# Router of a two-block network on one core: tokens split before the norm's root is known, the root applied per expert slot

## The chip, the cores and the metric

One NeuronCore of a Trainium2 chip runs the whole network in one launch. The metric is device time in microseconds (us) of that launch. The engines that matter here are TensorE (PE; its weight loads are PEld), VectorE (DVE), ScalarE (ACT), GpSimd (POOL) and SyncE (SP), whose queue issues the weight transfers.

## The reference, cut to what matters

A first network block (two layers) and a hybrid attention layer run over 256 tokens of width 1024; then comes a mixture of experts with 32 experts of hidden width 512, two per token, and a last norm. Only the way into the experts is touched:

```python
def rms_norm_2(x, g):
    y = x * lax.rsqrt(jnp.mean(x * x, axis=-1, keepdims=True) + RMS_EPS)
    return y * g

x = x + mixed @ w_out
x = x + hier_moe(rms_norm_2(x, g_ffn), ...)

def hier_moe(xt, ...):
    g_logit = xt @ w_group + b_group            # 4 groups: the best one is taken
    e_logit = xt @ w_expert + b_expert          # 8 experts in it: the best two are taken
    ...
    hid = jax.nn.silu(xb @ w1[e]) * (xb @ w3[e])
    out = hid @ w2[e]                           # weighted by the gate, summed per token
```

The norm's factor (the reciprocal root) is one number per token, so it can be applied to the logits and to the products with w1 and w3 in place of the tokens themselves.

## The kernel before

**Stages.** The tokens stand in two halves b = 0, 1 of 128 tokens, one per partition; `h` is the residual. The output projection (`work`, three fp32r matmuls per product, L122 to L124) fills four PSUM banks `accs[b][n]`, n being the half of the 1024 columns. Then, per half of the tokens: `half(b, n)` adds the bank to `h`, squares it (ACT) and multiplies by the norm's gain into `ys[b]` (GpSimd for n = 0, VectorE for n = 1); `scale(b)` makes the reciprocal root `rs[b]`; `turned(b, n)` transposes `ys[b]` and copies it to `yT` (ACT, L1210); `logits(b, n)` multiplies by the router's weights; `choose(b)` picks the two experts in twelve VectorE instructions (L1184 to L1195); `kept(b)` puts `h` back into the PSUM banks; and `place(b)` splits the normed tokens into a high and a low part `xs[0]`, `xs[1]` (tiles `xt`): the high part on ACT (L1237), the low part on GpSimd (L1242). ACT, VectorE and GpSimd run these in the order in which the code calls them (`ordered`). After `choose(1)` come the ranks within each expert (five small matmuls), `rank`, and the experts.

**Experts.** `pairs` goes over 16 pairs of experts, each expert with 64 slots. `where` compares ranks and makes the one-hot `oh` (L1392); `gather` multiplies `xs` by it into `xg` (PE, L1407); `up` multiplies by w1 and w3 (L1420), `silu` and `product` (L1352) give `hid`, `turn` transposes it (L1356), `down` multiplies by w2 (L1438), `collect` adds the result to the tokens (L1445). `slots` transposes the gates (L1426) into `GT` and the slot's gate `gs`. All engines but SP run this in the written order (`in_order`).

**Weights.** Each pair needs six loads of 2048 KB (two of w1, w3, w2 each), all issued by SP in order. They go to eleven slots (names `mw` and `w`); the twelfth load takes the place of the first one, so it waits until the matmuls of `up` with the first tile are done. Load number k+11 in general waits for the last reader of load k.

Of the kernel before, what the change touches and what calls it, by code (L numbers as in the profile page):

```python
# [56 lines left out]
class Net:  # L57
# [1108 lines left out]
    def to_moe(self):  # L1166
# [30 lines left out]
        def go(accs, work):  # L1197
# [20 lines left out]
            def half(b, n):  # L1218
                sl = slice(n * 512, (n + 1) * 512)
                yield v.tensor_add(h[:, b, sl], h[:, b, sl], accs[b][n])  # L1220
                self.square(h[:, b, sl], ss[b], n)
                yield (nc.gpsimd, v)[n].tensor_mul(ys[b][:, sl], h[:, b, sl], self.gp[:, sl])
# [3 lines left out]
            def kept(b):  # L1226
                for n in range(2):
                    nc.tensor.matmul(accs[b][n], self.ident, h[:, b, n * 512:(n + 1) * 512], start=True, stop=False)

            def scale(b):  # L1230
                yield self.rstd_begin(ss[b])
                yield rs.append(self.rstd_end(ss[b]))
# [17 lines left out]
            with self.ordered():  # L1250
                run(half(0, 0))
                run(half(0, 1))
                run(scale(0))
                for n in range(2):
# [91 lines left out]
    def silu(self, h1, hid):  # L1346
# [3 lines left out]
    def product(self, h3, hid):  # L1350
        hv = hid.rearrange("q c p -> q p c")
        self.nc.vector.tensor_mul(hv, hv, h3.rearrange("q (p c) -> q p c", c=4))  # L1352
# [27 lines left out]
    def pairs(self, ps):  # L1380
# [42 lines left out]
        def slots(q, og):  # L1423
# [3 lines left out]
            GT, gs = self.t(self.ex, (T,), FR, "GT", 2), self.small(1, "gs", bufs=2)  # L1427
            v.tensor_scalar(GT, gp, 0.0, None, op0=OP.is_gt)
            v.reduce_sum(gs, gp, axis=AX.X)
            return GT, gs  # L1430
# [16 lines left out]
        before = None  # L1447
        oh, xg = where(ps[0] // 2), A((8, 256), "xg")
        if ps[0] == 0:
            self.gates(A((4, 128), "hT")[:, 0, :64])  # L1450
            self.spill(A((4, 128), "hid")[:, 0, :64].rearrange("p (r e) -> p r e", r=2))
        og = gated(ps[0] // 2, oh)
        for p in ps:
            g, q = divmod(p, 2)
            more = q == 1 and p != ps[-1]
            if more:
                oh = where(g + 1)
            hid, hT = A((4, 128), "hid"), A((4, 128), "hT")
# [35 lines left out]
    def overflowing(self, wt, ps, oh, og, xg, hid, hT):  # L1494
# [5 lines left out]
        rs, gs, i2 = self.small(2), self.small(2), self.small(8, "i2", I32, 1)  # L1500
# [233 lines left out]
```

## Time and profile before

| | us |
|---|---|
| median of 3 runs (1306.73 to 1308.27) | 1306.81 |
| the profiled execution's own time | 1308.52 |
| its span, first to last instruction | 1306.7 |
| busy: PE / DVE / ACT / POOL | 1242.1 / 692.2 / 598.9 / 169.2 |

The 1.8 us between the span and the execution's own time lie outside the program's instructions. PE is counted busy while a matmul waits in its pipeline too, so its share does not say that PE is the limit everywhere. The output projection ends and the router starts at about 836 us of the span; the experts take from about 859 to 1296 us.

### The profile page before, as it was taken

To read this page: it belongs to the slowest core of one execution; us is meant where nothing else is said; L and a number is where in the kernel's file an instruction comes from. 1 tells how busy PE (TensorE), PEld (TensorE's weight loads), DVE (VectorE), ACT (ScalarE), POOL (GpSimd) and SP (SyncE) were. 2 spreads that over 40 slices of the span, in tenths; PEclk is the share of its full clock that TensorE was granted. 3 is DMA by queue.
4 is the path that set the end of the run, shared out by engine and by line. 5 is a ranking of instruction groups with operands and counts; after the bars stand their busy time and mean duration, and the time that the engine had idled before them with its cause. 6 is when DMAs were issued, how large, how long until landed. Compare 5 with 4: busy or idle time off the path is not lost. (4 is left out here: it accounts for less than half of the span.)

```text
span 1306.7 us, 19148 instructions
## 1 busy us (share of the span) xinstructions
PE 1242.1 (95%) x7647; PEld 922.7 (71%) x7647; DVE 692.2 (53%) x1396; ACT 598.9 (46%) x1113; POOL 169.2 (13%) x174
## 2 busy tenths in 40 slices
PE   7899999999999999999989999979999999989896
PEld 6787999997997899998888899734344343433332
DVE  5778977776787887777578645641111111111112
ACT  5667655555776755556445655431111111111103
POOL 4101000003021000001564511310000000000000
PEclk9999999999999999999989999989999999999999
DMA  9544555393452475344523375789999999999995
GB/s 370 220 160 147 199 190 183 107 339 118 161 194 81 149 257 194 130 159 141 210 78 117 130 257 201 288 326 414 427 427 428 427 427 427 428 426 427 427 423 228
DMA packets 93175, 341.05 MB, mean 261 GB/s; under 512 B 6972, under 2 KB 14108, under 8 KB 69788
## 3 DMA queue, kind: packets, MB, share of 16 engines
q1 hardware_dynamic: 91680, 336.87, 65.4%
q10 hardware_dynamic: 1404, 2.93, 0.7%
q8 instruction: 61, 1.00, 0.3%
q14 instruction: 30, 0.25, 0.0%
HBM read 338.75 MB, written 1.05 MB: 260 GB/s over the span
## 5 line engine op out<-in xcount | busy, mean ns | idle before, releaser
L122 PE MATMUL ps<-xt,wh 128*128 128x256 f32 x1072 | 303.0, 283 | 0.0
L124 PE MATMUL ps<-xt,wl 128*128 128x256 f32 x1072 | 300.6, 280 | 0.2 <-DVE wl L117 0.2
L123 PE MATMUL ps<-xt,wh 128*128 128x256 f32 x1072 | 300.2, 280 | 0.0
L117 DVE TENSOR_TENSOR wl<-w,wh 128x1024 fp32r<-128x1024 f32 (+3 forms) x193 | 228.0, 1187 | 96.3 <-ACT wh L116 95.0
L116 ACT ACTIVATE wh<-w 128x1024 fp32r<-128x1024 f32 (+2 forms) x196 | 197.2, 1014 | 164.9 <-PE ps L123 130.8
L122 PEld LDWEIGHTS ps<-xt,wh 128*128 128x128 f32 x1072 | 202.0, 188 | 4.0 <-issue 1.4
L123 PEld LDWEIGHTS ps<-xt,wh 128*128 128x128 f32 x1072 | 202.1, 189 | 1.9
L124 PEld LDWEIGHTS ps<-xt,wl 128*128 128x128 f32 x1072 | 201.9, 188 | 1.1 <-DVE wl L117 0.6
L1420 PE MATMUL ps<-mw,xg 128*64 128x512 f32 x592 | 132.3, 597 | 5.3 <-DMA mw<-in_w_dram 5.3
L1352 DVE TENSOR_TENSOR hid<-hid,ps 128x512 f32<-128x512 f32 x16 | 17.1, 1068 | 217.0 <-PE ps L1420 198.7
L1420 PEld LDWEIGHTS ps<-mw,xg 128*64 128x64 f32 x592 | 42.4, 138 | 91.0 <-issue 80.7
L1440 DVE SCALAR_TENSOR_TENSOR ys<-ps,gs,ys 128x512 fp32r<-128x512 f32 x32 | 24.0, 751 | 152.7 <-ACT ys L1439 152.7
L1420 PE MATMUL ps<-w,xg 128*64 128x512 f32 x432 | 96.3, 594 | 6.5 <-DMA w<-in_w_dram 6.5
L226 POOL TENSOR_TENSOR nu<-h,gain 128x512 f32<-128x512 f32 x18 | 25.7, 1450 | 428.6 <-DVE h L298 367.4
L1420 PEld LDWEIGHTS ps<-w,xg 128*64 128x64 f32 x432 | 30.7, 137 | 69.6 <-issue 58.5
L1439 ACT ACTIVATE ys<-ps,gs 128x512 fp32r<-128x512 f32 x32 | 22.0, 687 | 106.4 <-PE ps L1438 106.4
L124 PE MATMUL ps<-dh,hT 128*128 128x512 f32 x176 | 69.4, 394 | 0.0
L122 PE MATMUL ps<-dh,hT 128*128 128x512 f32 x176 | 69.3, 396 | 0.0
L123 PE MATMUL ps<-dl,hT 128*128 128x512 f32 x176 | 68.7, 391 | 0.0
L1357 ACT ACTIVATE hT<-ps 128x512 f32<-128x512 f32 x16 | 9.6, 598 | 126.2 <-PE ps L1356 126.1
L116 ACT ACTIVATE dh<-w 128x1024 fp32r<-128x1024 f32 x44 | 46.1, 1056 | 45.7 <-PE ps L124 44.0
L117 DVE TENSOR_TENSOR dl<-w,dh 128x1024 fp32r<-128x1024 f32 x44 | 53.8, 1223 | 22.4 <-ACT dh L116 22.4
(413 smaller groups left out, 2195.9 us busy)
## 6 DMA issues: line engine op xcount, KB each, us to landing
mw<-in_w_dram SPq DMA_DIRECT2D x49, 2048.0 KB, 28.8
w<-in_w_dram SPq DMA_DIRECT2D x41, 2048.0 KB, 27.2
w<-in_ffn_w_up_dram SPq DMA_DIRECT2D x20, 2048.0 KB, 7.9
w<-in_w_in_dram SPq DMA_DIRECT2D x11, 2048.0 KB, 7.4
w<-in_ffn_w_down_dram SPq DMA_DIRECT2D x10, 2048.0 KB, 7.7
w<-in_diff_w_qkv_dram SPq DMA_DIRECT2D x6, 2048.0 KB, 8.1
mw<-in_w_dram SPq DMA_DIRECT2D x6, 1024.0 KB, 18.3
w<-in_mla_w_o_dram SPq DMA_DIRECT2D x2, 2048.0 KB, 16.6
```

Source lines behind the costliest of these rows:

```text
L116: self.nc.scalar.activation(v(hi), raw, AF.Copy)
L117: (eng or self.nc.vector).tensor_sub(v(lo), raw, v(hi).bitcast(FT))
L122: mm(out, a[0], b[0], start=start, stop=False)
L123: mm(out, a[0], b[1], start=False, stop=False)
L124: mm(out, a[1], b[0], start=False, stop=stop)
L226: x = eng[n].tensor_mul(w[n], self.h[:, b, sl], self.gp[:, sl])
L1352: self.nc.vector.tensor_mul(hv, hv, h3.rearrange("q (p c) -> q p c", c=4))
L1357: self.nc.scalar.activation(hT.rearrange("p c s -> p (c s)"), pt, AF.Copy)
L1420: mm(p[64 * z:64 * z + 64], xg[:, k, c0:c0 + 64], wt[k // 4][:, o:o + 512], start=k == 0, stop=k == 7)
L1439: nc.scalar.activation(ys[0][n], p, AF.Copy, scale=gs)
L1440: v.scalar_tensor_tensor(ys[1][n], p, gs, ys[0][n].bitcast(FT), op0=OP.mult, op1=OP.subtract)
```

## The change

The tokens are split without the root: `high` and `low` take `ys` (residual times gain) by halves of the columns, before the root is known, so `place` with its four long instructions goes away; `low` stands on VectorE for three of the four halves and on GpSimd for (0, 1). Only the router's logits get the root (in `choose`, as before). `choose(0)` now stands ahead of `half(1, 1)` on VectorE instead of behind and within it. The root is kept in `self.rstd`; `row_scales` spreads it over all partitions once (two small matmuls, tile `rb`), `row_scale` sums it per slot (VectorE, one instruction per pair), and `silu` and `product` multiply by it. `slots` is called one pair ahead, and for the first pair between the w1 and the w3 products.

```diff
-            def place(b):
-                yk = ys[b].rearrange("q (p k) -> q k p", k=8)
-                hi, lo = self.xs[0][:, b], self.xs[1][:, b]
-                nc.scalar.activation(hi, yk, AF.Copy, scale=rs[b])
-                if b:
-                    nc.scalar.activation(ys[b], ys[b], AF.Copy, scale=rs[b])
-                else:
-                    nc.gpsimd.tensor_scalar(ys[b], ys[b], rs[b], None, op0=OP.mult)
-                nc.gpsimd.tensor_sub(lo, yk, hi.bitcast(FT))
+            def part(b, n):
+                yk = ys[b][:, n * 512:(n + 1) * 512].rearrange("q (p k) -> q k p", k=8)
+                return [yk] + [x[:, b, :, 64 * n:64 * n + 64] for x in self.xs]
+
+            def high(b, n):
+                yk, hi, _ = part(b, n)
+                nc.scalar.activation(hi, yk, AF.Copy)
+
+            def low(b, n, eng):
+                yk, hi, lo = part(b, n)
+                eng.tensor_sub(lo, yk, hi.bitcast(FT))
...
-                run(half(0, 0))
-                run(half(0, 1))
-                run(scale(0))
-                for n in range(2):
-                    turned(0, n)
-                run(half(1, 0))
-                place(0)
+                half(0, 0)
+                half(0, 1)
+                high(0, 0)
+                turned(0, 0)
+                turned(0, 1)
+                half(1, 0)
+                low(0, 0, v)
+                scale(0)
+                high(0, 1)
                 work(1, (1,), (5,))
                 for n in range(2):
                     logits(0, n)
+                scaled(0)
+                run(choose(0, lp, rs[0]))
+                low(0, 1, nc.gpsimd)
                 turned(1, 0)
-                work(1, (1,), (6,))
+                high(1, 0)
+                work(1, (1,))
                 logits(1, 0)
-                work(1, (1,))
-                c0 = choose(0, lp, rs[0])
-                run(half(1, 1))
-                for _ in range(5):
-                    next(c0)
-                run(scale(1), c0)
-                kept(0)
+                kept(0, 0)
+                half(1, 1)
+                scale(1)
+                low(1, 0, v)
                 turned(1, 1)
+                scaled(1)
+                high(1, 1)
                 logits(1, 1)
-                kept(1)
-                place(1)
+                kept(0, 1)
+                for n in range(2):
+                    kept(1, n)
                 run(choose(1, lp, rs[1]))
+                low(1, 1, v)
...
+                self.rstd = self.small(2, "rstd", bufs=1)
+                for b in range(2):
+                    v.tensor_copy(self.rstd[:, b:b + 1], rs[b])
...
-        self.nc.scalar.activation(hv, h1.rearrange("q (p c) -> q p c", c=4), AF.Silu)
+        self.nc.scalar.activation(hv, h1.rearrange("q (p c) -> q p c", c=4), AF.Silu, scale=r)
...
-        self.nc.vector.tensor_mul(hv, hv, h3.rearrange("q (p c) -> q p c", c=4))
+        self.nc.vector.scalar_tensor_tensor(hv, h3.rearrange("q (p c) -> q p c", c=4), r, hv, op0=OP.mult, op1=OP.mult)
+
+    def row_scale(self, gT, r):
+        j = self.t(self.ex, (T,), BF, "rj", 1)
+        self.nc.vector.scalar_tensor_tensor(j, gT, 0.0, self.rb, op0=OP.is_gt, op1=OP.mult, accum_out=r)
+        return r
+
+    def row_scales(self, dg):
+        p = self.ps()[:, :T]
+        for b in range(2):
+            self.nc.vector.tensor_scalar(dg[:, b], self.ident, self.rstd[:, b:b + 1], None, op0=OP.mult)
+        self.nc.gpsimd.memset(dg[:, 2], 1.0)
+        for b in range(2):
+            self.nc.tensor.matmul(p[:, b * 128:(b + 1) * 128], dg[:, 2], dg[:, b], start=True, stop=True)
+        self.rb = self.t(self.ex, (T,), FT, "rb", 1)
+        self.nc.scalar.activation(self.rb, p, AF.Copy)
...
+            h1 = up(q, xg, oh if p == ps[0] else None)
+            if p == 0:
+                self.row_scales(dg)
+                self.spill(A((4, 128), "hT")[:, 0, :64].rearrange("p (r e) -> p r e", r=2))
+            if now is None:
+                now = slots(q, og)
+            GT, gs, r = now
...
+            if p != ps[-1]:
+                now = slots(1 - q, og)
             wt = self.weights()
```

Below is VectorE's queue around `half(1, 1)`, the add and the gain of the last quarter (L1220 and L1222, bank `ps_9334`, tile `y_1672`). First as it stood before:

```order
L1220 TENSOR_TENSOR h_88<-h_88,ps_9334 128x512
L1222 TENSOR_TENSOR y_1672_9311<-h_88,gain_6955 128x512
L1184 SCALAR_TENSOR_TENSOR lg_83<-ps_9425,sm_9429,br_8616 128x36
L1185 TENSOR_REDUCE gm_9321<-lg_83 128x1
L1186 SCALAR_TENSOR_TENSOR sm_9323<-lg_83,gm_9321,sm_9313 128x4
L1187 TENSOR_REDUCE sm_9318<-sm_9323 128x1
L1188 TENSOR_SCALAR sm_9324<-sm_9323,sm_9318 128x4
L161 TENSOR_SCALAR sm_9430<-sm_9430 128x1
```

The same place in the changed kernel, from the end of `choose(0)` on:

```order
L1194 TENSOR_SCALAR one_9316<-consts_92,sm_9326 128x32 x2
L1195 TENSOR_TENSOR asg_9315<-one_9316 128x32
L1220 TENSOR_TENSOR h_88<-h_88,ps_9334 128x512
L1222 TENSOR_TENSOR y_1672_9311<-h_88,gain_6955 128x512
L161 TENSOR_SCALAR sm_9430<-sm_9430 128x1
L165 TENSOR_SCALAR sm_9430<-sm_9430 128x1
L1246 TENSOR_TENSOR xt_1711_9428<-y_1672_9311,xt_1710_9427 128x8x64
L172 RECIPROCAL sm_9430<-sm_9430 128x1
L173 SCALAR_TENSOR_TENSOR sm_9430<-sm_9430 128x1
L174 SCALAR_TENSOR_TENSOR sm_9430<-sm_9430 128x1
L1184 SCALAR_TENSOR_TENSOR lg_83<-ps_9425,sm_9430,br_8616 128x36
```

The first token half's choice moved from behind the last quarter's add to ahead of it; `low(1, 0)` (L1246) is new between the two steps of the root.

The end of VectorE's router work, before; L1282 makes `rank`, L1392 the one-hot `oh`:

```order
L1194 TENSOR_SCALAR one_9316<-consts_92,sm_9326 128x32 x2
L1195 TENSOR_TENSOR asg_9315<-one_9316 128x32
L1282 SCALAR_TENSOR_TENSOR rank_81<-ps_9426,asg_9315 128x64
L1392 TENSOR_TENSOR oh_9615<-rank_81,consts_92 128x256 x2
L1293 TENSOR_TENSOR sm_9620<-lg_83,gm_9321 128x8
```

And in the changed kernel, where the rank is on L1293 and the one-hot on L1421:

```order
L1194 TENSOR_SCALAR one_9316<-consts_92,sm_9326 128x32 x2
L1195 TENSOR_TENSOR asg_9315<-one_9316 128x32
L1246 TENSOR_TENSOR xt_1711_9428<-y_1672_9311,xt_1710_9427 128x8x64
L1293 SCALAR_TENSOR_TENSOR rank_81<-ps_9426,asg_9315 128x64
L1299 COPY rstd_9587<-sm_9429 128x1
L1299 COPY rstd_9587<-sm_9430 128x1
L1421 TENSOR_TENSOR oh_9620<-rank_81,consts_92 128x256 x2
```

`low(1, 1)` and two copies of the root came in between the choice and the one-hot.

TensorE's queue in the first pair of experts, before, from the second half of the w1 product to the first w2 product:

```order
L1420 MATMUL ps_9658<-mw_8608,xg_9618 64x512 x8
L1420 MATMUL ps_9720<-w_9716,xg_9618 64x512 x8
L1420 MATMUL ps_9720<-w_9718,xg_9618 64x512 x8
L1426 MATMUL ps_9738<-consts_92,og_9653 128x128 x2
L1356 MATMUL ps_9745<-consts_92,hid_9656 128x128 x4
L1438 MATMUL ps_9755<-w_9751,hT_9657 64x512 x4
```

And in the changed kernel (L1449 is the `up` matmul, L1455 the gates' transpose, L1385 that of `hid`, L1468 the `down` matmul):

```order
L1449 MATMUL ps_9646<-mw_8608,xg_9623 64x512 x8
L1379 MATMUL ps_9703<-hid_9642 128x128 x2
L1455 MATMUL ps_9727<-consts_92,og_9643 128x128 x2
L1449 MATMUL ps_9744<-w_9740,xg_9623 64x512 x8
L1449 MATMUL ps_9744<-w_9742,xg_9623 64x512 x8
L1385 MATMUL ps_9762<-consts_92,hid_9737 128x128 x4
L1455 MATMUL ps_9768<-consts_92,og_9643 128x128 x2
L1468 MATMUL ps_9782<-w_9778,hT_9738 64x512 x4
```

Two matmuls of the root (L1379) are new ahead of the w3 product, the gates' transposes moved there from behind it, and those of the next pair came in ahead of `down`.

## Rows read from the trace of the kernel before

**Rows 1.** Windows: a stretch of the expert stage, with the view's columns.

```profile
core 0: us, PE busy (x) PEld busy (x) DVE busy (x) ACT busy (x) POOL busy (x), PEclk, DMA share, GB/s
1200.00:1250.00 50.00, 44.58 (x219) 18.23 (x220) 5.50 (x9) 7.83 (x11) 3.31 (x4) 1.00 1.01 427
```

**Rows 2.** Windows of 2 us around the start of the experts, same columns.

```profile
854.00:856.00 2.00, 0.00 (x0) 0.00 (x0) 1.93 (x5) 1.82 (x2) 1.38 (x1) 0.53 1.03 438
...
862.00:864.00 2.00, 2.00 (x8) 0.92 (x8) 1.76 (x10) 0.60 (x1) 0.88 (x2) 0.50 0.00 0
864.00:866.00 2.00, 2.00 (x10) 0.56 (x8) 0.06 (x1) 0.00 (x0) 0.00 (x0) 0.91 0.00 0
...
888.00:890.00 2.00, 2.00 (x14) 0.59 (x10) 0.00 (x0) 0.65 (x1) 0.00 (x0) 1.00 0.89 320
```

**Rows 3.** Timeline of SP's queue: start, us from first to last issue, loads.

```profile
846.92 20.61 SPq L1339 DMA_DIRECT2D mw<-in_w_dram  x2
...
876.28 11.71 SPq L1337 DMA_DIRECT2D w<-in_w_dram  x3
```

**Rows 4.** Chain that ended last, in order of time: start, us, what.

```profile
1121.53 32.80 DMA w<-in_w_dram
...
1286.93 0.22 PE ps L1426 x2
```

**Rows 5.** Timeline, all engines, from the last quarter's add to the experts.

```profile
845.44 0.69 DVE L1220 TENSOR_TENSOR h<-h,ps 128x512 f32<-128x512 f32 x1 [5.08 <-PE ps L124]
846.17 0.69 DVE L1222 TENSOR_TENSOR y<-h,gain 128x512 f32<-128x512 f32 x1
846.51 3.05 POOL L1242 TENSOR_TENSOR xt<-y,xt 128x1024 fp32r<-128x1024 f32 x1
847.25 2.33 DVE L1186 SCALAR_TENSOR_TENSOR sm<-lg,gm,sm 128x4 f32<-128x4 f32 x1
850.39 0.58 ACT L1210 ACTIVATE yT<-ps 128x512 f32<-128x512 f32 x1
851.02 1.08 PE L1214 MATMUL ps<-wr,yT 128*128 128x36 f32 x8 [1.67 <-ACT yT L1210]
852.28 0.25 DVE L1184 SCALAR_TENSOR_TENSOR lg<-ps,sm,br 128x36 f32<-128x36 f32 x1
852.76 0.22 DVE L1186 SCALAR_TENSOR_TENSOR sm<-lg,gm,sm 128x4 f32<-128x4 f32 x1
854.44 3.06 DVE L1194 TENSOR_SCALAR one<-consts,sm 128x32 bf16<-128x32 f32 x2
854.62 2.84 POOL L1242 TENSOR_TENSOR xt<-y,xt 128x1024 fp32r<-128x1024 f32 x1 [5.05 <-ACT y L1239]
857.53 0.17 DVE L1195 TENSOR_TENSOR asg<-one 128x32 bf16<-128x32 bf16 x1
858.36 0.76 DVE L1392 TENSOR_TENSOR oh<-rank,consts 128x256 fp32r<-128x256 f32 x2
858.93 3.75 PE L1407 MATMUL ps<-oh,xt 128*128 128x256 f32 x16 [0.93 <-DVE oh L1392]
862.62 4.50 PE L1420 MATMUL ps<-mw,xg 128*64 128x512 f32 x16
```

**Rows 6.** Timeline of the same kernel, PE and ACT, just ahead of that.

```profile
840.63 1.87 PE L1214 MATMUL ps<-wr,yT 128*128 128x36 f32 x16
...
841.29 2.19 ACT L1237 ACTIVATE xt<-y,sm 128x1024 fp32r<-128x1024 f32 x1
...
844.93 0.48 PE L124 MATMUL ps<-wh,mix 128*128 128x512 f32 x1
```

**Rows 7.** Groups of instructions by line and form: busy us, mean ns.

```profile
L1352 DVE TENSOR_TENSOR hid<-hid,ps 128x512 f32<-128x512 f32 x16 | 17.1, 1068 | 217.0 <-PE ps L1420 198.7 <-issue 18.2
L1242 POOL TENSOR_TENSOR xt<-y,xt 128x1024 fp32r<-128x1024 f32 x2 | 5.9, 2946 | 5.1 <-ACT y L1239 5.1
```

**Rows 8.** Timeline of PE in the first pair, the gates' transposes.

```profile
879.60 0.44 PE L1426 MATMUL ps<-consts,og 128*128 128x128 f32 x2
```

More of the change, by code (lines that the diff above doesn't have):

```diff
@@ L1219, in half, with kept, scaled, run @@
                 sl = slice(n * 512, (n + 1) * 512)
-                yield v.tensor_add(h[:, b, sl], h[:, b, sl], accs[b][n])
+                v.tensor_add(h[:, b, sl], h[:, b, sl], accs[b][n])
                 self.square(h[:, b, sl], ss[b], n)
-                yield (nc.gpsimd, v)[n].tensor_mul(ys[b][:, sl], h[:, b, sl], self.gp[:, sl])
+                (nc.gpsimd, v)[n].tensor_mul(ys[b][:, sl], h[:, b, sl], self.gp[:, sl])
             self.accs = accs
-            def kept(b):
-                for n in range(2):
-                    nc.tensor.matmul(accs[b][n], self.ident, h[:, b, n * 512:(n + 1) * 512], start=True, stop=False)
+            def kept(b, n):
+                nc.tensor.matmul(accs[b][n], self.ident, h[:, b, n * 512:(n + 1) * 512], start=True, stop=False)
             def scale(b):
-                yield self.rstd_begin(ss[b])
-                yield rs.append(self.rstd_end(ss[b]))
-            def place(b):
-                yk = ys[b].rearrange("q (p k) -> q k p", k=8)
-                hi, lo = self.xs[0][:, b], self.xs[1][:, b]
-                nc.scalar.activation(hi, yk, AF.Copy, scale=rs[b])
-                if b:
-                    nc.scalar.activation(ys[b], ys[b], AF.Copy, scale=rs[b])
-                else:
-                    nc.gpsimd.tensor_scalar(ys[b], ys[b], rs[b], None, op0=OP.mult)
-                nc.gpsimd.tensor_sub(lo, yk, hi.bitcast(FT))
-            def run(*gs):
-                for _ in itertools.zip_longest(*gs):
+                self.rstd_begin(ss[b])
+                self.root(ss[b])
+            def scaled(b):
+                rs.append(self.rstd_end(ss[b], True))
+            def part(b, n):
[7 more added lines that the diff above has]
+                eng.tensor_sub(lo, yk, hi.bitcast(FT))
+            def run(g):
+                for _ in g:
                     pass
@@ L1344, in wslot, with silu, product @@
         return t
-    def silu(self, h1, hid):
+    def silu(self, h1, hid, r):
         hv = hid.rearrange("q c p -> q p c")
-        self.nc.scalar.activation(hv, h1.rearrange("q (p c) -> q p c", c=4), AF.Silu)
-    def product(self, h3, hid):
+        self.nc.scalar.activation(hv, h1.rearrange("q (p c) -> q p c", c=4), AF.Silu, scale=r)
+    def product(self, h3, hid, r):
         hv = hid.rearrange("q c p -> q p c")
-        self.nc.vector.tensor_mul(hv, hv, h3.rearrange("q (p c) -> q p c", c=4))
+        self.nc.vector.scalar_tensor_tensor(hv, h3.rearrange("q (p c) -> q p c", c=4), r, hv, op0=OP.mult, op1=OP.mult)
[12 more added lines that the diff above has]
+        self.nc.scalar.activation(self.rb, p, AF.Copy)
     def turn(self, hid, hT, pt):
@@ L1426, in slots @@
                 nc.tensor.transpose(gp[:, b * 128:(b + 1) * 128], og[:, b, 2 * q:2 * q + 2].rearrange("p e s -> p (e s)"), self.ident)
-            GT, gs = self.t(self.ex, (T,), FR, "GT", 2), self.small(1, "gs", bufs=2)
+            GT, gs, r = self.t(self.ex, (T,), FR, "GT", 2), self.small(1, "gs", bufs=2), self.small(1, "rg", bufs=2)
+            self.row_scale(gp, r)
             v.tensor_scalar(GT, gp, 0.0, None, op0=OP.is_gt)
             v.reduce_sum(gs, gp, axis=AX.X)
-            return GT, gs
+            return GT, gs, r
         def down(hT, wt, n, gs, last):
@@ L1445, in collect @@
                     mm(accs[b][n], GT[:, b * 128:(b + 1) * 128], ys[x][n], start=False, stop=last and x == 1)
-        before = None
+        before, now = None, None
         oh, xg = where(ps[0] // 2), A((8, 256), "xg")
@@ L1450, in pairs @@
             self.gates(A((4, 128), "hT")[:, 0, :64])
-            self.spill(A((4, 128), "hid")[:, 0, :64].rearrange("p (r e) -> p r e", r=2))
+            dg = A((4, 128), "hid")
         og = gated(ps[0] // 2, oh)
@@ L1457, in pairs @@
                 oh = where(g + 1)
+                og = gated(g + 1, oh)
+            h1 = up(q, xg, oh if p == ps[0] else None)
[5 more added lines that the diff above has]
+            GT, gs, r = now
             hid, hT = A((4, 128), "hid"), A((4, 128), "hT")
-            h1 = up(q, xg, oh if p == ps[0] else None)
-            self.silu(h1, hid)
+            self.silu(h1, hid, r)
             h3 = up(q, xg, None)
-            self.product(h3, hid)
+            self.product(h3, hid, r)
             if before:
@@ L1499, in overflowing @@
         tmp, t2 = hT[:, 0, :32], [self.small(8) for _ in range(2)]
-        rs, gs, i2 = self.small(2), self.small(2), self.small(8, "i2", I32, 1)
+        rs, gs, i2, r = self.small(2), self.small(2), self.small(8, "i2", I32, 1), self.small(1)
         e = nc.sync.value_load(ei[0:1, 0:1], min_val=0, max_val=31)
@@ L1528, in overflowing @@
                 mm(ps[z], xg[:, k], wt[z][:, k * 512:(k + 1) * 512], start=k == 0, stop=k == 7)
-        self.silu(ps[0], hid)
-        self.product(ps[1], hid)
+        self.silu(ps[0], hid, r)
+        self.product(ps[1], hid, r)
         self.turn(hid, hT, ps[3])
```

5 lines of the change are left out of this document (1 added, 4 removed).

## Prediction

> **What bounds the kernel now.** I read the windows of the last third first. While the experts run, the DMA share is 1.01 and 427 GB/s arrive [rows 1]: the weights' transfers are the limit, and TensorE, busy 44.58 of 50 us there, waits for them in the end. The chain of waits says how far ahead the loads are: one issued at 1121.53 landed 32.80 us later, where a load of 2048 KB takes 4.9 us at 427 GB/s, so several stood in line and a late release of one slot cost nothing [rows 4]. From such a point on the end is fixed by bytes over rate. What can move it is a hole in the transfers before the line has formed.
>
> Windows of 2 us find it: nothing moves from 862 to 866 us [rows 2]. SP's queue says why. It issued the eleventh load at 846.92 and the twelfth 20.61 - 0.37 us later (the last issue itself takes 0.37), at 867.16 [rows 3]. The twelfth takes the place of the first, which TensorE reads in its first w1 product from 862.62 for 4.50 us [rows 5]. So **whatever brings the first gather and that product forward by x us brings all later loads, and the end, forward by x**, as long as the eleven loads are not themselves late: they end at about 862, some 5 us ahead of the release.
>
> The timeline gives the path there [rows 5]. The last quarter's add on VectorE starts at 845.44, once the output projection's last matmul (844.93 + 0.48) is done [rows 6]; the gather starts at 858.93, 13.49 us later. Two VectorE steps stick out: L1186, 0.22 us at 852.76, took 2.33 at 847.25, and the pair L1194 took 3.06. Both end with an L1242 of GpSimd, 846.51 + 3.05 and 854.62 + 2.84. The first of them also held back the root on ACT, and behind it the copy L1210: y of the quarter was done at 846.86 and its copy began only at 850.39.
>
> **The change, part by part.** All times count from T, the start of the last quarter's add, which is 845.44 before.
>
> *Where T goes.* `choose(0)` now stands ahead of that add, so T is its end. The logits of the first half are done at 840.63 + 1.87 = 842.5 [rows 6]. L1184 and L1185 follow (0.25 and about as much), so L1186 is due at about 843.1. `low(0, 1)` on GpSimd becomes ready at the same time: ACT was free for L1237 at 841.29 and now does there the root (0.3, an estimate from the one-column steps of these rows) and `high(0, 1)`, half of 2.19; the other `high` ahead of it mostly fills idle time: about 843.0. GpSimd then runs half of L1242's 2946 ns [rows 7], 1.5 us, to 844.5. I expect VectorE to be held again for that time. What is left of `choose(0)` behind L1186 is, in `choose(1)` of before, 854.44 - 852.98 = 1.46 up to L1194, 0.4 for its pair unheld (two such as L1186) and 0.17, so 2.05 us [rows 5]. T is about 846.6, **1.15 us later** than before. Bounds: 846.0 if L1186 gets in first, 847.6 under the second rival.
>
> *From T to the gather.* y of the quarter is done at T + 1.42 as before (846.17 + 0.69 - 845.44). The root no longer waits behind L1186, so the four transposes (0.22 each [rows 8], so 0.9) and the copy (0.58) give T + 2.9, the logits (1.08) T + 4.0. `low(1, 0)` on VectorE lies beside this: no row shows a VectorE subtraction with this stride; its bounds are 0.69 (plain 512 columns, L1222) and 1.07 (L1352, 512 columns with a stride) [rows 5, 7]. I take 1.07, since both are strided; the root is then done at T + 3.7, still ahead of the logits, so it costs nothing. `choose(1)` unheld takes 852.98 - 852.28 = 0.70 and 2.05, so T + 6.8; GpSimd has nothing to do there. New on the path: `low(1, 1)`, 1.07 (bounds as above), and two copies of one column (0.17 each, as L1195, the shortest row). The ranks' matmuls hide behind `low(1, 1)`. With the rank (0.25) that is T + 8.5 for the one-hot, and the gather starts 858.93 - 858.36 = 0.57 after it: **T + 9.1 in place of T + 13.49, 4.4 us shorter**. With T the gather starts at about 855.7, 3.2 us earlier. The gather and the first product are not changed, so the release of the first slot moves by the same 3.2.
>
> *The clock.* TensorE idles from the last logits (851.02 + 1.08) to 858.93 but for five small matmuls; the granted clock is 0.53 in 854 to 856 and still 0.50 in 862 to 864, then 0.91 [rows 2], so it fell to the lower level (1.2 GHz) in the gap and came back about 5.4 us after the gather began. The gap is now 5.1 us (T + 4.0 to T + 9.1), shorter, so I expect it to fall again, with a slow stretch of work that is 0 to 1 us shorter, worth half of it: 0.4 with some rounding up.
>
> *Given back in the first pair.* Between the w1 and the w3 products TensorE now also does the two root matmuls and two gate transposes. The transposes are 0.44 [rows 8]; the matmuls of the same size 0.25 to 0.6, I take 0.4. The transposes that follow `turn` lie beside ACT's copy of `hid`. So `down` ends 0.8 us later relative to the gather. That counts: the third load of the group at 876.28 was issued at its end, 887.6 [rows 3], it waits for the first slot that `down` frees, and DMA already sags there, to 320 GB/s in 888 to 890 [rows 2]. The line has not formed yet. **0.8 us lost.** The loads in front have 3 us of cover or more, since the DMA is behind them.
>
> *Nothing elsewhere.* In later pairs VectorE does one more instruction of 256 columns and a three-operand product; it is busy for 5.50 of 50 us in the expert stage [rows 1], and SP has loads in line [rows 4]. If that cover were gone each pair would cost up to about 0.5 us. At the end of the last pair the gates' transposes are gone from between the w3 product and `turn`: 0.22 gained [rows 4].
>
> *Sum.* 4.4 - 1.15 + 0.4 - 0.8 + 0.2 = 3.05, so 3.0 us less. The profiled execution took 1308.52 (span 1306.7), 1.7 over the median of 1306.81; both should move alike: 1305.5 for such an execution, **1303.8 as the median**.
>
> **The rivals.**
> (1) *The clock stays up or returns early.* For it: the gap is 1.7 us shorter. Against: a gap of 5.1 us is still long. The first gathers (3.75 us at half clock) and the start of the product (4.50) would save up to 2.4 us in all [rows 5], 2.0 beyond my 0.4: 1301.8.
> (2) *VectorE and GpSimd meet once more.* The new subtractions read two SBUF tiles, and `low(0, 0)` is due just as GpSimd starts the gain of (1, 0). If GpSimd is first, the subtraction, the root behind it and `choose(0)` slip by about 0.9; if the subtractions cost more than 1.07, some tenths more. Gain 1.6 to 2.1: 1305.0. The Trainium skill, page "SBUF — State Buffer", section "Who interferes with whom", says that a VectorE instruction with two SBUF inputs and a GpSimd instruction that reads SBUF exclude each other, the first to start holding for its whole length. By that rule the change brings one meeting of this kind back into `choose(0)` and a second into `low(0, 0)`; the trace agrees as far as L1186 shows it, 2.33 us for 0.22. Without the rule, with GpSimd free for VectorE, T would be near 845.3 and the gain about 4.
> (3) *No change.* The w3 product waits for the new root work (VectorE's scaling of the identity, GpSimd's fill), some 3 us in place of 0.8. Against it: both are due some 10 us before the w1 product ends. 1306.8.
> (4) *Slower.* `low(0, 1)` on GpSimd takes far longer in its new three-level form than half of L1242, and holds VectorE and with it T. My sum is used up when it takes 4.5 us, and the kernel is slower by 0.2% from 7.1 on; at 8 us it would be 1310.3. L1242 with the same stride speaks against it.
>
> **How the numbers follow.** About 0.2%, 2.6 us, is what a measurement of this kernel can tell from no change. Forecast 45% (its own range 1302.9 to 1304.9; some two thirds of it are over 2.6 us of gain), rival 1 18%, rival 2 22%, rival 3 8%, rival 4 7%. Faster is 0.30 from the forecast, 0.18 from rival 1 and 0.04 from the better end of rival 2: 0.52. Same is the rest of the forecast and of rival 2 and rival 3: 0.41. Slower is rival 4, 0.07. The range of 8 in 10 runs from 1301.6 (the clock and plain-price subtractions) to 1306.3 (most of rival 2 and a part of rival 3).
>
> **What would show it.** In the profile after: the first gather at about 855.7 and the twelfth issue at about 863.7; no VectorE step of the router over 1.1 us behind T; one of `choose(0)` held until GpSimd's `low(0, 1)` ends; T near 846.6; a low clock until about 5 us after the gather begins; the w3 product 0.8 us behind the w1 product; DMA at 427 GB/s from about 890 to the end. I am wrong if the gather comes forward and the twelfth issue does not, or if both do and holes open in DMA after 890.

## The result, and the profile after

The changed kernel takes 1315.13 us (median of 4 runs, 1313.84 to 1316.02) and the kernel before 1306.77 (4 runs, 1306.08 to 1308.27): a ratio of 1.0065, 95% interval 1.0053 to 1.0078. It is slower by 0.65%, outside the range of the forecast. The profiled execution shown here took 1313.84 (span 1312.1). It is the fastest of its four, and that of the kernel before, 1308.52, is slower than all four of its kernel, so the two traces differ by 5.3 us where the medians differ by 8.4.

The timeline of the changed kernel around the router answers to [rows 5]. L1246 is `low`, L1186 the step of four columns, L1436 the gather, L1449 the product:

```profile
840.84 0.69 DVE L1220 TENSOR_TENSOR h<-h,ps 128x512 f32<-128x512 f32 x1 [0.82 <-PE ps L124]
...
847.52 1.63 POOL L1246 TENSOR_TENSOR xt<-y,xt 128x512 fp32r<-128x512 f32 x1 [0.58 <-ACT xt L1242]
848.11 1.07 DVE L1186 SCALAR_TENSOR_TENSOR sm<-lg,gm,sm 128x4 f32<-128x4 f32 x1
...
851.14 0.68 DVE L1220 TENSOR_TENSOR h<-h,ps 128x512 f32<-128x512 f32 x1
...
855.61 0.22 DVE L1186 SCALAR_TENSOR_TENSOR sm<-lg,gm,sm 128x4 f32<-128x4 f32 x1
...
857.79 1.06 DVE L1246 TENSOR_TENSOR xt<-y,xt 128x512 fp32r<-128x512 f32 x1
...
859.59 3.75 PE L1436 MATMUL ps<-oh,xt 128*128 128x256 f32 x16 [1.43 <-DVE oh L1421]
863.27 4.11 PE L1449 MATMUL ps<-mw,xg 128*64 128x512 f32 x16
```

From T, the start of the last quarter's add (851.14), to the gather it is 8.45 us, where 13.49 were before and 9.1 forecast. So the router did what it should. Yet the gather starts at 859.59, later than before. The first line says why: the router's first add stands at 840.84. Before, the same row was:

```profile
836.01 0.69 DVE L1220 TENSOR_TENSOR h<-h,ps 128x512 f32<-128x512 f32 x1 [0.83 <-PE ps L124]
```

So 4.83 us were lost ahead of the router, in code that the diff does not touch. SP's queue in the changed kernel (start, us from first to last issue, loads; answers to [rows 3]):

```profile
852.61 15.19 SPq L1353 DMA_DIRECT2D mw<-in_w_dram  x2
...
877.56 11.78 SPq L1351 DMA_DIRECT2D w<-in_w_dram  x3
...
1307.06 2.06 SPq L1609 DMA_DIRECT2D out_dram<-mw  x4
```

The twelfth load went out at 852.61 + 15.19 - 0.37 = 867.43, and the output's first store at 1307.06. Before, that store stood at

```profile
1301.90 2.07 SPq L1572 DMA_DIRECT2D out_dram<-mw  x4
```

| us | before | changed | difference |
|---|---|---|---|
| router's first add | 836.01 | 840.84 | +4.83 |
| from there to the twelfth load | 31.15 | 26.59 | -4.56 |
| from there to the output's store | 434.74 | 439.63 | +4.89 |
| sum: output's store | 1301.90 | 1307.06 | +5.16 |

The third part is the expert stage. Its windows (answer to [rows 1]) show no hole; the share of DMA time is 1.01 as before, but fewer bytes arrive:

```profile
1200.00:1250.00 50.00, 44.60 (x220) 18.90 (x218) 8.11 (x16) 7.46 (x11) 3.36 (x4) 1.00 1.01 421
900.00:1250.00 350.00, 333.89 (x1638) 139.85 (x1636) 52.48 (x103) 56.30 (x79) 9.52 (x14) 1.00 1.01 421
```

421 GB/s in place of 427: over some 430 us that is 430 x (427/421 - 1) = 6.1 us, enough for the 4.89 lost there. What the diff changes for code that it does not touch is where the tiles lie. The tiles `rstd` and `rg` (two buffers) take three slots of 32 bytes in the pool of small tiles, and every pool opened behind it on the same side of SBUF moves by 96 bytes; those opened with `side="right"`, among them the residual and the split weights of the first block, stay. From the built programs, the first byte of SBUF of some tiles:

```
                       before   changed   e1       e2       f2
first w slot             4096      4192     4192     4096     4352
xt (matmuls read it)    86016     86112    86112    86016    86272
first mw slot          102400    102496   102496   102400   102656
multiple of 256 bytes     yes        no       no      yes      yes
```

### The profile page after: what moved, and what is told of

It is laid out like the page before. It is cut to its first block, busy times and chain, and to the rows that moved or that the text cites. A ratio compares the mean times of both kernels' runs of the same rounds, so it can differ in the third digit from the quotient of the medians.

```text
span 1312.1 us, 19205 instructions
## 1 busy us (share of the span) xinstructions
PE 1248.9 (95%) x7651; PEld 929.5 (71%) x7651; DVE 698.6 (53%) x1435; ACT 599.1 (46%) x1115; POOL 160.6 (12%) x173
## 5 line engine op out<-in xcount | busy, mean ns | idle before, releaser
L122 PE MATMUL ps<-xt,wh 128*128 128x256 f32 x1072 | 306.6, 286 | 0.0
L124 PE MATMUL ps<-xt,wl 128*128 128x256 f32 x1072 | 304.3, 284 | 0.2
L123 PE MATMUL ps<-xt,wh 128*128 128x256 f32 x1072 | 304.0, 284 | 0.0
L123 PEld LDWEIGHTS ps<-xt,wh 128*128 128x128 f32 x1072 | 202.8, 189 | 1.6
L124 PEld LDWEIGHTS ps<-xt,wl 128*128 128x128 f32 x1072 | 202.8, 189 | 1.0 <-DVE wl L117 0.6
L1449 PE MATMUL ps<-mw,xg 128*64 128x512 f32 x592 | 131.9, 596 | 6.0 <-DMA mw<-in_w_dram 6.0
L1366 DVE SCALAR_TENSOR_TENSOR hid<-ps,rg,hid 128x512 f32<-128x512 f32 x16 | 17.9, 1120 | 196.9 <-PE ps L1449 196.9
L1449 PEld LDWEIGHTS ps<-mw,xg 128*64 128x64 f32 x592 | 42.3, 137 | 90.8 <-issue 80.2
L1449 PE MATMUL ps<-w,xg 128*64 128x512 f32 x432 | 96.4, 594 | 7.4 <-DMA w<-in_w_dram 7.4
L1449 PEld LDWEIGHTS ps<-w,xg 128*64 128x64 f32 x432 | 30.5, 137 | 70.1 <-issue 57.9
L124 PE MATMUL ps<-dh,hT 128*128 128x512 f32 x176 | 68.8, 391 | 0.0
L123 PE MATMUL ps<-dl,hT 128*128 128x512 f32 x176 | 68.6, 390 | 0.0
```

The costliest lines, as they stand in the source:

```text
L122: mm(out, a[0], b[0], start=start, stop=False)
L123: mm(out, a[0], b[1], start=False, stop=False)
L124: mm(out, a[1], b[0], start=False, stop=stop)
L1366: self.nc.vector.scalar_tensor_tensor(hv, h3.rearrange("q (p c) -> q p c", c=4), r, hv, op0=OP.mult, op1=OP.mult)
L1449: mm(p[64 * z:64 * z + 64], xg[:, k, c0:c0 + 64], wt[k // 4][:, o:o + 512], start=k == 0, stop=k == 7)
```

## Experiments

Line numbers differ by one or more between these kernels. One table has all timed runs: median, ratio to the kernel before, run beside it on the same chip (its medians there: 1306.28 to 1307.44), with its interval, and from the profiled execution the router's first add, the time from there to the twelfth load, from there to the output's store, and GB/s in 900 to 1250.

| | us | ratio | first add | to 12th | to store | GB/s |
|---|---|---|---|---|---|---|
| before | 1306.77 | 1 | 836.01 | 31.15 | 434.74 | 427 |
| changed | 1315.13 | 1.0065 (1.0053, 1.0078) | 840.84 | 26.59 | 439.63 | 421 |
| e1 before, all 96 off | 1318.17 | 1.0082 (1.0068, 1.0096) | 841.48 | 30.45 | 439.88 | 421 |
| e2 changed, old places | 1302.71 | 0.9966 (0.9954, 0.9978) | 836.30 | 26.81 | 434.81 | 427 |
| e3 before, all 64 off | 1321.39 | 1.0111 (1.0096, 1.0127) | 843.69 | 30.14 | 440.65 | 421 |
| e4 changed, all 128 off | 1314.14 | 1.0047 (1.0033, 1.0060) | 839.53 | 26.26 | 442.60 | 421 |
| f2 before, all 256 off | 1306.77 | 0.9998 (0.9989, 1.0007) | 836.14 | 30.56 | 433.92 | 427 |
| f3 e2, `low(0, 1)` on VectorE | 1303.24 | 0.9970 (0.9959, 0.9980) | 834.49 | 26.45 | 434.06 | 427 |
| f4 e2, `low(1, 1)` on GpSimd | 1302.89 | 0.9966 (0.9955, 0.9977) | 835.46 | 26.64 | 434.83 | 427 |
| g1 changed, all 256 off | 1303.66 | 0.9969 (0.9957, 0.9981) | 836.04 | 26.85 | 433.93 | 427 |
| h1 before, w slots 96 off | 1308.14 | 1.0007 (0.9998, 1.0016) | 836.20 | 30.40 | 435.61 | 426 |
| h2 before, xt 96 off | 1311.57 | 1.0027 (1.0016, 1.0038) | 840.28 | 31.72 | 434.68 | 427 |
| h3 before, all behind xt 96 off | 1308.00 | 1.0003 (0.9994, 1.0012) | 834.83 | 30.65 | 436.76 | 425 |
| i1 before, all but xt 96 off | 1310.65 | 1.0035 (1.0021, 1.0048) | 833.85 | 30.61 | 440.82 | 421 |
| i2 before, xt and w slots 96 off | 1312.04 | 1.0050 (1.0036, 1.0064) | 838.70 | 29.85 | 436.00 | 426 |

The first add moves with TensorE's granted clock ahead of the router. Over 0 to 100 us and 600 to 700 us that was 1.00 and 0.98 in the traces of the changed kernel, e1, e4, h3 and i1, 1.00 and 1.00 in f3 and i2, 0.98 and 0.98 in the others (0.97 in before); elsewhere up to 834 us it was 1.00 in all. In the kernels whose xt lies at a multiple of 256 bytes the first add is at 833.85 to 834.83 in the first two groups and at 835.46 to 836.30 in the third. So first adds are best compared within a group.

**e1: the kernel before, the tiles behind the small pool 96 bytes further, as in the changed kernel.**

```diff
         nc.gpsimd.memset(self.eps, EPS)
+        nc.gpsimd.memset(self.small(24, "pad", bufs=1), 0.0)
```

> The kernel before, with one unused small tile of 96 bytes in the pool that stands ahead of the weight tiles in SBUF (and one memset of it at the start). Nothing else differs, but every tile behind that pool now lies 96 bytes further, as in the changed kernel, where the new small tiles (root, slot's root) took the same 96 bytes. Theory A (the place of the tiles makes the transfers longer): 421 GB/s in place of 427 in the expert stage, several us lost ahead of the router already, and 1306.8 + 4.8 (lost ahead of the router) + 5.7 (lost from the twelfth load on) = about 1317 us. Theory B (the chip or its memory ran slower in that session, or the new instructions disturb the transfers): 427 GB/s and 1306.8 us, no difference.

1318.17, 10.8 us slower, with nothing of the change in it. Theory A holds: 5.5 us are lost ahead of the router, 5.1 behind the twelfth load. Its window:

```profile
900.00:1250.00 350.00, 332.47 (x1634) 140.31 (x1632) 46.57 (x77) 56.20 (x80) 9.14 (x16) 1.00 1.01 421
```

**e2: the changed kernel, tiles at their old places.**

```diff
-        self.p1 = self.small(2, "p1", bufs=1)
+        pr = self.small(4, "p1", bufs=1)
+        self.p1, self.rstd = pr[:, :2], pr[:, 2:]
...
-                self.rstd = self.small(2, "rstd", bufs=1)
...
-            GT, gs, r = self.t(self.ex, (T,), FR, "GT", 2), self.small(1, "gs", bufs=2), self.small(1, "rg", bufs=2)
+            GT, gr = self.t(self.ex, (T,), FR, "GT", 2), self.small(2, "gs", bufs=2)
+            gs, r = gr[:, 0:1], gr[:, 1:2]
```

> The changed kernel, with the root kept in two spare columns of an existing small tile (that of p1) and the slot's root in a second column of the tile of the gate's sum, so that the pool is as large as before and all weight tiles stand at their places of before. Instructions and their order are those of the changed kernel. Theory A (place of the tiles): 427 GB/s again, no drift ahead of the router, and the gain of the router comes out; there the sixteenth load was issued 3.5 us earlier, counted from the router's start, so about 1303.3 us, near the forecast of 1303.8. Theory B (the new instructions disturb the transfers): 421 GB/s and about 1315 us.

1302.71: faster than before by 0.34%, 12.4 us faster than the change as it was. The whole loss was that of the places. In its timeline the first add stands where it stood before, T is 846.63 and the gather 3.84 us earlier than before:

```profile
836.30 0.69 DVE L1221 TENSOR_TENSOR h<-h,ps 128x512 f32<-128x512 f32 x1 [0.82 <-PE ps L124]
...
842.99 1.66 POOL L1247 TENSOR_TENSOR xt<-y,xt 128x512 fp32r<-128x512 f32 x1 [0.60 <-ACT xt L1243]
843.56 1.11 DVE L1187 SCALAR_TENSOR_TENSOR sm<-lg,gm,sm 128x4 f32<-128x4 f32 x1
...
846.63 0.68 DVE L1221 TENSOR_TENSOR h<-h,ps 128x512 f32<-128x512 f32 x1
...
855.09 3.75 PE L1436 MATMUL ps<-oh,xt 128*128 128x256 f32 x16 [1.43 <-DVE oh L1421]
```

Its windows, with the granted clock in the column ahead of the DMA share:

```profile
857.00:859.00 2.00, 2.00 (x11) 1.78 (x12) 1.83 (x11) 0.72 (x2) 1.15 (x2) 0.50 1.03 438
859.00:861.00 2.00, 2.00 (x8) 0.58 (x8) 1.31 (x8) 0.48 (x1) 0.30 (x2) 0.72 0.95 401
861.00:863.00 2.00, 2.00 (x11) 0.42 (x7) 0.00 (x0) 0.00 (x0) 0.00 (x0) 1.00 0.03 12
...
900.00:1250.00 350.00, 336.78 (x1650) 141.13 (x1650) 52.48 (x103) 57.49 (x80) 9.53 (x14) 1.00 1.01 427
```

**e3 and e4: which multiple counts.** As e1 with `self.small(16, "pad", bufs=1)`, and the changed kernel with `self.small(8, "pad", bufs=1)`.

> As the run with 96 bytes, but the unused tile has 64 bytes, so that all tiles behind it begin at a multiple of 64 bytes and not at one of 128. Theory A1 (what counts is a multiple of 64): 427 GB/s and 1306.8 us. Theory A2 (a larger multiple counts, 128 to 512): 421 GB/s and about 1317 us. Theory B (place is nothing): 1306.8 us, told from A1 by the run with 96 bytes alone.

> The changed kernel with 32 unused bytes more in the small pool, so that the weight tiles lie 128 bytes behind their places of before: a multiple of 128, not of 256. Theory A1 (64 bytes count): 427 GB/s and about 1303.3 us, as at the old places. Theory A2 (a multiple of 256 or more counts): about 1315 us as the changed kernel. If the two are alike with 1306.8, the gain of the router is lost somewhere else.

Neither a multiple of 64 nor one of 128 is enough: 421 GB/s in both. That e3 lost 7.7 us ahead of the router and e1 only 5.5 was not expected. Much of it is the granted clock: against traces of their own group it is 7.6 us in e3 (843.69 against f2's 836.14) and 6.6 to 7.6 in e1 (841.48 against 834.83 in h3 and 833.85 in i1). That e3 is 3.2 us slower than e1 in time stays open, and so does the expert stage of e4, some 3 us longer than in the changed kernel at the same 421 GB/s.

**f1: the transfers alone.**

```diff
+    for o in (0, 96, 0, 64, 32, 128, 256, 384, 512, 1024, 2048, 0):
+        for i in range(10):
+            load(big[i][:, o // 4:o // 4 + 4096], i // 2, i % 2)
```

> A kernel that computes nothing: it only loads, again and again, the same ten pieces of the expert weights (2048 KB each, the same form as the kernel's own loads) into ten tiles that begin at multiples of 4096 bytes of SBUF, and writes zeros out; its time is of no interest, only the rate. Twelve groups of ten loads; in each group the data goes to another place in the tiles: 0, 96, 0, 64, 32, 128, 256, 384, 512, 1024, 2048 and 0 bytes behind the multiple of 4096. Theory A (the place that a transfer writes sets its length): 427 GB/s at 0, some 421 at 96, 64, 32 and 128, and the groups at 256, 384, 512 tell which multiple is enough. Theory C (the place matters only to the engines that use the tiles, or to transfers beside busy engines): one rate in all groups.

The run is one execution. A window of 40 us in each group, in that order (GB/s in the last column):

```profile
core 0: us, POOL busy (x), PEclk, DMA share, GB/s
8.00:48.00 40.00, 0.00 (x0) 1.00 1.01 428
57.00:97.00 40.00, 0.00 (x0) 1.00 1.01 423
107.00:147.00 40.00, 0.00 (x0) 1.00 1.01 428
156.00:196.00 40.00, 0.00 (x0) 1.00 1.01 423
205.00:245.00 40.00, 0.00 (x0) 1.00 1.01 421
254.00:294.00 40.00, 0.00 (x0) 1.00 1.01 422
304.00:344.00 40.00, 0.00 (x0) 1.00 1.01 428
353.00:393.00 40.00, 0.00 (x0) 1.00 1.01 423
402.00:442.00 40.00, 0.00 (x0) 1.00 1.01 428
452.00:492.00 40.00, 0.00 (x0) 1.00 1.01 428
501.00:541.00 40.00, 0.00 (x0) 1.00 1.01 428
550.00:590.00 40.00, 0.00 (x0) 1.00 1.01 428
```

0, 256, 512, 1024 and 2048 bytes: 428. 32, 64, 96, 128 and 384: 421 to 423. No engine computes beside it, so theory C is out. The Trainium skill, page "SBUF — State Buffer", section "Who interferes with whom", says that a DMA never contends with a compute engine; this run needs no such contention to show the loss.

**f2 and g1: 256 bytes.** The kernel before with `self.small(64, "pad", bufs=1)`, and the changed one with `self.small(40, "pad", bufs=1)` (96 + 160 = 256).

> The kernel before with an unused small tile of 256 bytes, so that all tiles behind it begin at an odd multiple of 256 bytes. If a multiple of 256 is enough: 427 GB/s and 1306.8 us. If 512 or more is wanted: 421 GB/s and 1317 to 1321 us, as with 96 and with 64 bytes.

> The changed kernel as it is, with 160 unused bytes more in the small pool, so that with the 96 bytes of its own new tiles every tile behind the pool lies 256 bytes further than before, at an odd multiple of 256 bytes. If only a multiple of 256 is wanted, the loss is gone without touching the change: 427 GB/s in the expert stage and some 1302.7 us, as with the tiles at their old places. If the new tiles cost something in another way, between 1304 and 1315 us.

1306.77 (ratio 0.9998) and 1303.66 (0.9969): 256 is enough, and one line of padding mends the change.

**f3: `low(0, 1)` on VectorE**, on the kernel of e2.

```diff
-                low(0, 1, nc.gpsimd)
...
+                low(0, 1, v)
                 low(1, 0, v)
```

> The changed kernel with the weight tiles at their old places (as e2), and low(0, 1) on VectorE, just ahead of low(1, 0), in place of GpSimd. If GpSimd's subtraction is what holds the instruction of four columns in choose(0) for 1.11 us, that one takes 0.22 and the start of the last quarter's add comes 0.9 us earlier, counted from the router's start; the root then ends some 0.4 us behind the logits, so the gather comes 0.4 to 0.5 us earlier. If the hold has another cause, the add is not earlier and the gather comes 0.4 us later. In time too little to be told: 1302 to 1303 us.

The step that took 1.11 in e2 is short, and T stands 9.43 us behind the first add (834.49) in place of 10.33, the 0.90 expected:

```profile
841.73 0.22 DVE L1187 SCALAR_TENSOR_TENSOR sm<-lg,gm,sm 128x4 f32<-128x4 f32 x1
...
843.92 0.68 DVE L1221 TENSOR_TENSOR h<-h,ps 128x512 f32<-128x512 f32 x1
...
853.05 3.75 PE L1436 MATMUL ps<-oh,xt 128*128 128x256 f32 x16 [1.43 <-DVE oh L1421]
```

The gather comes 18.56 behind the first add, in e2 18.79: 0.2 earlier, half of what was expected.

**f4: `low(1, 1)` on GpSimd**, on the kernel of e2: GpSimd is no longer idle during the last choice.

```diff
-                low(1, 1, v)
+                low(1, 1, nc.gpsimd)
```

> The changed kernel with the weight tiles at their old places (as e2), and low(1, 1) on GpSimd in place of VectorE, which undoes that GpSimd is idle during the last choice. If GpSimd and VectorE exclude each other there, a VectorE instruction of choose(1) is held for about 0.9 us until the subtraction of 1.66 us on GpSimd ends, and of the 1.06 us that VectorE saves only 0.2 come out at the gather. If they don't, the gather comes 1.06 us earlier. In time too little to be told: 1302 to 1303 us.

```profile
849.66 1.51 POOL L1247 TENSOR_TENSOR xt<-y,xt 128x512 fp32r<-128x512 f32 x1 [5.89 <-ACT xt L1243]
850.22 0.97 DVE L1187 SCALAR_TENSOR_TENSOR sm<-lg,gm,sm 128x4 f32<-128x4 f32 x1
...
854.45 3.75 PE L1436 MATMUL ps<-oh,xt 128*128 128x256 f32 x16 [0.92 <-DVE oh L1421]
```

The step is held until GpSimd ends, for 0.97 us in place of 0.22. The gather comes at 854.45, 18.99 behind the first add (835.46), 0.2 later than in e2 and not the 0.2 earlier that was expected: the rank's matmuls, hidden behind `low(1, 1)` in e2, now stand on the path with 0.33. The same section of the Trainium skill says that a VectorE instruction with two SBUF inputs and a GpSimd one that reads SBUF exclude each other; by f3 and f4 the trace agrees, with 0.9 and 0.75 us of hold that come and go with GpSimd's subtraction. For the time it is a wash.

**h1, h2, h3: which tiles.** A tile is said to lie well when it begins at a multiple of 256 bytes, and badly when not. The kernel before with 96 bytes ahead of some tiles, and 160 behind them where others follow, so that the rest lies well: only the w slots lie badly (h1), only xt (h2), only what stands behind xt (h3). The edit of h2 follows; h3 has its second part alone, with 24 in place of 40, and h1 the two lines that are shown for i1 and i2:

```diff
+        nc.gpsimd.memset(self.t(self.xp, (24,), FT, "pada", 1), 0.0)
...
+        x = [self.t(self.xp, (8, T), FR, f"xt{i}", 1) for i in range(2)]
+        if not self.filler:
+            self.filler = self.t(self.xp, (40,), FT, "padb", 1)
+            self.nc.gpsimd.memset(self.filler, 0.0)
```

> The kernel before with the 96 unused bytes ahead of the five w slots, and 160 more behind them, so that only the w slots lie badly; xt, the tiles of all stages and the six mw slots lie 256 bytes further, which cost nothing in f2. Theory D (the loss ahead of the router, some 5 us, is that of transfers too; all weights of the first block go to w slots): 5 us there and 5 of 11 parts of the 5.7 us in the expert stage, 2.6: about 1314.5 us. Theory E (the loss ahead of the router is TensorE's: its matmuls of 256 columns on xt took 284 to 286 ns in the mean with 96 bytes, 280 to 283 before): only the 2.6: about 1309.6 us.

> The kernel before with 96 unused bytes ahead of the two xt tiles and 160 behind them, so that only xt, which the matmuls of the first block read, lies 96 bytes off; the w slots lie as before, everything behind xt 256 bytes further. Theory D: 1307.0 us, and the 3192 matmuls of 256 columns at 280 to 283 ns. Theory E: they take 284 to 286 ns as in e1, some 5 us are lost ahead of the router, and the time is about 1312 us.

> The kernel before with 96 unused bytes behind the xt tiles, so that w slots and xt lie as before, and all tiles of the stages and the six mw slots 96 bytes off. Theories D and E alike: nothing ahead of the router, and 6 of 11 parts of the 5.7 us in the expert stage, 3.1: about 1310 us. More than that would say that other engines' work on the tiles of the stages pays too.

In time h1 and h3 don't differ from the kernel before beyond their intervals; h2 is 4.1 us slower (2.1 to 5.0 by the interval). h2 speaks for theory E: with xt alone badly placed, the loss is all ahead of the router (first add at 840.28; in the kernels whose xt lies well it is at 833.85 to 836.30), at an unchanged 427 GB/s. The groups by line and form (busy us, mean ns) of the matmuls that read xt, of the kernel before, then of h2, then of e1:

```profile
L122 PE MATMUL ps<-xt,wh 128*128 128x256 f32 x1064 | 300.8, 283 | 0.0
```

```profile
L122 PE MATMUL ps<-xt,wh 128*128 128x256 f32 x1064 | 302.8, 285 | 0.0
```

```profile
L122 PE MATMUL ps<-xt,wh 128*128 128x256 f32 x1064 | 304.3, 286 | 0.0
```

L123 and L124 went from 280 to 282 in h2 and to 284 in e1. So 3192 matmuls of 256 columns are 2 ns longer in the mean when the xt that they read lies badly, some 6 us of busy time, of which 4.1 come out. That is half of the lengthening that theory E expected (284 to 286). It is not a few long matmuls: in the trace the median from the start of one to the start of the next is 117 ns before, 119 in h2 and 120 in e1. Theory D fails for the part ahead of the router: h1, where all w slots lie badly, has its first add at 836.20.

Behind the twelfth load h1 lost 0.9 us and h3 2.0, where shares of 5.7 us made 2.6 and 3.1. The trace's packets say why. Mean ns of the packets of 8192 bytes of each load, in order of issue from 1002 us on in h3 (a few packets over 600 ns left out); there the mw slots lie badly and the w slots well:

```
mw 309.2  w 309.1  w 309.0  mw 309.0  mw 309.1  mw 312.0  mw 314.1  mw 313.9  w 309.4  w 309.0
```

In e1 every load has 314 there. A bad load is not slow at once: the first two or so behind a good one take 309 like good ones, and only then 314. In f1 it is the same: of the ten loads of each bad group that follows a good one (96, 64 and 384 bytes) the first two take 309; those groups read 423, the two that follow a bad one 421 and 422. Windows of h3, first over the well placed loads and the two bad ones behind them, then over the last three:

```profile
1002.00:1026.00 24.00, 24.00 (x130) 11.66 (x128) 3.33 (x5) 5.44 (x8) 1.19 (x2) 1.00 1.01 428
1029.00:1042.00 13.00, 13.00 (x64) 5.24 (x62) 3.14 (x5) 1.97 (x3) 0.00 (x0) 1.00 1.01 422
```

**i1 and i2: do the parts act together?**

```diff
+        nc.gpsimd.memset(self.small(24, "pad", bufs=1), 0.0)
+        nc.gpsimd.memset(self.t(self.xp, (40,), FT, "pada", 1), 0.0)
```

with 24 in place of 40 behind xt is i1; i2 has the first line alone and 40 behind xt.

> The kernel before with 96 unused bytes ahead of the w slots, 160 between them and xt, and 96 behind xt: w slots, mw slots and the tiles of the stages lie 96 bytes off a multiple of 256, xt alone on one. In h1 and h3, where loads to good and to bad slots take turns, the packets of a bad load took 309 ns as long as a good one stood shortly ahead of it, and 314 only from the second or third bad load in a row on; so the two parts did not add up. Theory F (a row of bad loads alone is slow): here all loads of the expert stage are bad, 421 GB/s there, 5.5 us lost behind the twelfth load, nothing ahead of the router, 1313 us. If the parts just add up (0.7 and 0.6 us): 425 GB/s and 1308.7 us.

> The kernel before with 96 unused bytes ahead of the w slots and 160 behind xt: w slots and xt lie badly, the mw slots and the stages 256 bytes further. Theory G (matmuls that read a badly placed xt lose still more when the loads beside them go to badly placed slots): the 3192 matmuls of 256 columns take 284 to 286 ns as in e1, the loss ahead of the router is over 5 us, and the time is 1313 us. If the two don't act together: 282 to 285 ns as in h2, 4.2 us ahead of the router and 0.7 behind it, 1312 us.

i1: 421 GB/s again and 4.4 us slower (2.7 to 6.3 by the interval). Its trace shows 6.1 us lost behind the twelfth load, and a first add at 833.85, earlier than any; theory F holds, since its 5.5 us lie in the interval and the 1.3 of the sum of parts does not. i2: the matmuls at 282 to 284 ns as in h2, and the first add at 838.70, 4.2 us behind that of f3 with the same granted clock, as h2's is 4.1 behind f2's: theory G is not borne out. xt (4.1) and the rest (4.4) make 8.5 of the 10.8 us of e1 (8.9 to 12.5). By the times, whose intervals are wider than that, the 2.3 us left are not shown. By the traces something is left ahead of the router: 6.6 to 7.6 us are lost there in e1 and 4.1 in h2, and e1's matmuls take 1 to 2 ns more than with xt alone badly placed. Why stays open.

## Why the prediction was wrong

**The step that failed** is the one headed "Nothing elsewhere", and with it the sentence that the end "is fixed by bytes over rate" at 427 GB/s. Both take the rest of the program as unchanged, since its instructions are, and the sum has no term at all for the 836 us ahead of the router. The tiles were not unchanged: three new slots of 32 bytes moved xt and all weight slots off a multiple of 256 bytes, and that cost some 12.4 us (1315.13 less the 1302.71 of e2). In the traces it is 4.89 us behind the twelfth load and 4.83 ahead of the router, or 6.0 to 7.0 there against h3 and i1, whose granted clock was alike. None of the four rivals was of this kind. The holes in DMA after 890, by which I meant to see an error, did not come. The sign that failed was the 427 GB/s from 890 on: the transfers stayed dense and became longer, at 421.

**The mechanism itself was right**, as e2 and g1 show, with 1302.71 and 1303.66 us where 1303.8 was forecast. By the ratios the gain is 4.4 us in e2 (2.9 to 6.0) and 4.1 in g1 (2.5 to 5.6), where the sum had 3.0. Its terms, in e2:

| term | forecast | measured |
|---|---|---|
| T later | 1.15 | 0.90 (846.63 - 836.30 against 845.44 - 836.01) |
| T to the gather shorter | 4.4 | 5.03 (8.46 against 13.49) |
| clock, gather to the twelfth load | 0.4 | 0.21 (8.02 against 8.23) |
| given back in the first pair, less the tail | 0.6 | 0.07 (434.81 against 434.74) |

g1 repeats the first two rows (10.34 us from the first add to T, 8.46 from there to the gather), and they make 5.03 - 0.90 = 4.1 by themselves. The third row is not told from the scatter: from the gather to the twelfth load it is 8.23 before and 7.74 in f2, which has the same instructions.

T came as argued, by a hold of 1.11 us where some 1.4 were forecast. The path to the gather is 0.6 shorter than I made it. Most of that is the end: I priced the rank and the two copies of the root at 0.25 and 2 x 0.17, one behind the other. In e2 the copies run between the rank and the one-hot:

```profile
854.28 0.21 DVE L1294 SCALAR_TENSOR_TENSOR rank<-ps,asg 128x64 f32<-128x64 f32 x1
854.41 0.20 DVE L1299 COPY p<-sm 128x1 f32<-128x1 f32 x2
854.53 0.75 DVE L1421 TENSOR_TENSOR oh<-rank,consts 128x256 fp32r<-128x256 f32 x2
```

From the rank's start to the one-hot's it is 0.25 us with the copies, and it was 0.32 before without them, when the one-hot came straight behind the rank:

```profile
858.04 0.22 DVE L1282 SCALAR_TENSOR_TENSOR rank<-ps,asg 128x64 f32<-128x64 f32 x1 [0.33 <-PE ps L1281]
```

So the copies cost nothing. The clock fell again to the lower level and came back some 5 us after the gather began (0.50, 0.72, 1.00 in e2's windows), so rival 1 did not come. Nor did rival 2: `low(0, 0)` got in ahead of GpSimd's gain, which was the one delayed. Nor rival 3: in e2 the w3 product starts at 869.54, 0.8 us behind the end of the w1 product. Nor rival 4: `low(0, 1)` took 1.66 us on GpSimd.

The 0.8 us given back in the first pair are there. SP's queue in e2:

```profile
848.10 15.38 SPq L1353 DMA_DIRECT2D mw<-in_w_dram  x2
...
873.23 11.78 SPq L1351 DMA_DIRECT2D w<-in_w_dram  x3
...
1297.92 2.07 SPq L1610 DMA_DIRECT2D out_dram<-mw  x4
```

From the twelfth load (848.10 + 15.38 - 0.37) to the sixteenth (873.23 + 11.78 - 0.37) it is 21.53 us, and 20.46 before [rows 3]. But they don't reach the end: from the sixteenth load to the store it is 413.3 us in e2 and 414.3 before. The other traces at 427 GB/s agree: 412.4, 412.5 and 413.3 in g1, f3 and f4, against 413.5 and 414.3 in f2 and h2, which have the instructions of before. I had called that place one where the line of loads has not formed yet; a load there that comes 1 us late cost nothing that could be seen.

## What to carry to other kernels

Before a change is costed by its instructions, compare where the tiles lie: a small tile more in an early pool moves everything behind it. When time is lost in code that was not touched, pad the kernel before by as many bytes and time it; that takes one run and separates the change from its side effect. Here the pad that brings these tiles back to a multiple of 256 bytes turned a loss of 0.65% into a gain of 0.31% (g1).

## What the runs showed of the hardware

- Loads of 2048 KB into tiles that begin at a multiple of 256 bytes of SBUF ran at 428 GB/s, and at 421 to 423 where they began 32, 64, 96, 128 or 384 bytes behind (f1); packets of 8192 bytes took 309 and 314 ns.
- That is not felt at once: where good and bad loads take turns, the first two bad ones or so take as long as good ones (h3, f1).
- Matmuls of 256 columns took 2 ns longer in the mean when the tile that they read lay 96 bytes off (h2, 280 to 282 for two of the three lines), and 3 to 4 when w slots, xt and everything behind them did (e1).
